# Attention: the causal mask folded into the row-maximum pass, the negated maxima built as diagonals and copied by ScalarE, and a last key block of 16

## The chip, the cores and the metric

The kernel runs on one core of one Trainium2 chip. The metric is the device time of one execution in microseconds (us), the median over the runs. The engines are TensorE (PE; its weight loads are PEld), VectorE (DVE), ScalarE (ACT), GpSimd (POOL) and SyncE (SP), which issues nearly all DMAs from one in-order queue.

## The reference

One layer of a decoder trunk on 1024 tokens plus 16 learned meta tokens (L = 1040, D_MODEL = 1024). An input projection feeds four branches whose gated outputs are summed and projected again. The change lies in the second branch, multi-head latent attention with 8 heads:

```python
k_pos = jnp.arange(lp)
def attend(args):
    qb, i = args
    s = jnp.einsum('bqhd,bkhd->bhqk', qb, k).astype(jnp.float32)
    q_pos = i * Q_BLOCK + jnp.arange(Q_BLOCK)
    s = jnp.where(k_pos[None, :] <= q_pos[:, None], s, -jnp.inf)
    p = jax.nn.softmax(s, axis=-1).astype(v.dtype)
    return jnp.einsum('bhqk,bkhd->bqhd', p, v)
```

Queries and keys have 96 features (64 plus a rotary part of 32), values 64. The softmax is causal; the output leaves out the 16 meta positions.

## The kernel before

The program has three stages. The first, up to about 658 us of the profile, is the input projection (tiles `ps_pa` to `ps_pd`, from split weights `A`, `S` and split inputs `B`, `T`), with the small branches pumped in beside it. The last of these is the norm task of the convolution branch (`lacc`, `cgt`, `bohi`, stores to `bo`). The second, from about 658 to 883 us, is attention together with the output projections of three branches as filler (tiles `ps_y`, operands `bo`, `whl`, `th`, results `m`). The third is the output projection (`ps_u`, `ps_o`).

All float32 matmuls are split into a high and a low part and made of three matmuls. One 512-column matmul moves 128x512.

Attention works on 16 pieces: 8 heads h, each in two halves c of 512 queries. For a piece, `maxima(h, c)` computes each row's maximum first: for four groups of 128 queries the scores of all visible keys in one or two blocks (`ps_s<-kt,qt`, from 144 to 456 columns), the triangular mask `maskS` added on the last 128 columns of the last block, a maximum per block into `mx`, and over the blocks into `mr` (128 queries x 4 groups). `mr` is transposed on PE and spread by a multiplication with `negd` (-1 on a diagonal of 4 groups, 0 elsewhere) into rows 96 to 99 of the query tile `qt`; the key tile `kt` has ones there. So `attend(h, c)` gets scores with the maximum already subtracted. It goes over blocks of 128 keys: three score matmuls (`ps_s<-qt,kt`, keys on the partitions), the mask `maskT` on the diagonal blocks, an exponential on ACT (`p`), a split into high and low (`pt`, ACT and POOL), three matmuls with the values into `ps_o`. The scores of both functions share four PSUM banks (`ps_s`). `ol` is the copy of `ps_o`, `l`, `lc`, `r`, `rb` the row sums' way through DRAM, `lcp` the reciprocals of the last head, which go over PE.

The order on each engine isn't written by hand. The program records its operations, and a list scheduler (`Plan.flush`) walks through them with a cost for each and issues, per engine, the ready operation of the highest priority whose buffers are free. The cost of a PE operation is a rule in `Plan.cost`; these costs set the order only, each engine then runs its own list in that order and waits on semaphores. `plan.ahead` shifts priorities, `plan.behind` holds loads back in the plan. `load_q` and `load_kv` load `qt`, `kt` and `vt`; for heads 0 and 1 the rotary part `kr` is loaded too.

All operations carry line 330 of the profile, where the recorded operations are issued, so the profile is read by tiles.

Of the kernel before, what the change touches and what calls it, by code (L numbers as in the profile page):

```python
# [21 lines left out]
F32 = mybir.dt.float32  # L22
# [171 lines left out]
class Plan:  # L194
# [76 lines left out]
    @staticmethod  # L271
    def cost(eng, op, outs, ins, pow_):
        def size(v):
            return math.prod(v.shape[1:])
        if op == "dma_start":
            v, w = outs[0], ins[0]
            n = math.prod(v.shape) * 4
            run = 4 * min(v.shape[-1], w.shape[-1])
            return {"SP": 450, "ACT": 350, "POOL": 1000}[eng], n * (0.0235 + 35 / run) / 16
        n = max(size(v) for v in outs + [v for v in ins if isinstance(v, View)])  # L280
        if eng == "PE":
            n = size(outs[0])
            return (max(108, n / 2.25 + 3) if op == "transpose" or ins[0].dtype != F32 else max(430, 1.7 * n)), 0
        if eng == "ACT":
            return 200 + 0.83 * n, 0
        if eng == "POOL":
            return (500 + 140 * n if pow_ else 80 + 2.4 * n), 0
        psum = any(isinstance(v, View) and v.buf.psum for v in outs + ins)
        if op == "reciprocal":
            return 150 + 8.5 * n, 0  # L290
        return 142 + (1.2 if op == "scalar_tensor_tensor" and not psum else 1.07) * n, 0
# [144 lines left out]
def trunk_kernel(ctx, tc, a):  # L436
# [816 lines left out]
    for d in range(4):  # L1253
# [2 lines left out]
    boM = [[cp.tile([P, 2, 512], F32R, name=f"boM{i}{c}") for i in range(4)] for c in range(2)]  # L1256
    m_ = [[mpair[c][d // 2][:, d % 2] for d in range(KD)] for c in range(2)]

    maskS = qk.tile([P, P], F32, name="maskS")
    POOL.memset(maskS, 0.0)  # L1260
    POOL.affine_select(out=maskS, in_=maskS, compare_op=ALU.is_ge, fill=NEG,
                       base=0, pattern=[[-1, P]], channel_multiplier=1)
    maskT = qk.tile([P, P], F32, name="maskT")
    POOL.memset(maskT, 0.0)
    POOL.affine_select(out=maskT, in_=maskT, compare_op=ALU.is_ge, fill=NEG,
                       base=0, pattern=[[1, P]], channel_multiplier=-1)

    negd = qk.tile([4, 4, P], F32, name="negd")
    POOL.memset(negd, -1.0)
    POOL.affine_select(out=negd, in_=negd, compare_op=ALU.is_equal, fill=0.0,  # L1270
                       base=0, pattern=[[-1, 4], [0, P]], channel_multiplier=1)
    NA = QK + 4
    qt = {}

# [22 lines left out]
    def maxima(h, c):  # L1297

        q_, k_ = qt[h, c], kt[h % 2]
        mx = at.tile([P, 4, 3], F32, tag="mx", bufs=2, name="mx")
        POOL.memset(mx, NEG)
        for r in range(4):
            nk = NM + P * (4 * c + r + 1)
            nb = -(-nk // 512)
            w_ = -(-nk // nb)
            w_ += w_ % 2
            n0 = 0  # L1310
            for b in range(nb):
                n = min(w_, nk - n0)
                s = bank("s")
                PE.matmul(s[:, :n], q_[:QK, 0, P * r:P * (r + 1)], k_[:QK, 0, n0:n0 + n], start=True, stop=True)
                if b == nb - 1:
                    add(DVE, s[:, n - P:n], s[:, n - P:n], maskS)
                DVE.tensor_reduce(mx[:, r, b:b + 1], s[:, :n], axis=AX.X, op=ALU.max)
                n0 += n
            yield
        mr = at.tile([P, 4], F32, tag="mr", bufs=2, name="mr")  # L1320
        DVE.tensor_reduce(mr, mx, axis=AX.X, op=ALU.max)
        pm = bank("s")
        PE.transpose(pm[:4, :P], mr, ident)
        DVE.tensor_tensor(q_[QK:NA, 0, :].rearrange("p (r n) -> p r n", n=P),
                          pm[:4, :P].unsqueeze(1).to_broadcast([4, 4, P]), negd, op=ALU.mult)
        yield

    ol = {}
# [1 line left out]
    def attend(h, c):  # L1330
# [4 lines left out]
        for j in range(nj):  # L1335
            lo_ = max(512 * c, P * j - NM)
            n = 512 * (c + 1) - lo_
            kn = P if j < 8 else NM
            ks = slice(P * j, P * j + kn)
            qs = slice(512 - n, 512)  # L1340
            s = bank("s")[:kn, :n]
            PE.matmul(s, k_[:NA, 0, ks], q_[:NA, 0, qs], start=True, stop=False)
            PE.matmul(s, k_[:QK, 0, ks], q_[:QK, 1, qs], start=False, stop=False)
            PE.matmul(s, k_[:QK, 1, ks], q_[:QK, 0, qs], start=False, stop=True)
            d0 = P * j - NM
            dl, dh = max(d0, 512 * c, 0), min(d0 + P, 512 * (c + 1))
            if dh > dl:
                sd = s[:, dl - lo_:dh - lo_]
                add(DVE, sd, sd, maskT[:kn, dl - d0:dh - d0])
            p32 = at.tile([P, 512], F32, tag="p32", bufs=3, name="p32")[:kn, :n]  # L1350
            pt_ = at.tile([P, 2, 512], F32R, tag="pt", bufs=4, name="pt")[:kn, :, :n]
            ACT.activation(p32, s, AF.Exp)
            split(pt_[:, 0], pt_[:, 1], p32)
            o = po[:, lo_ - 512 * c:]
            PE.matmul(o, v_[:kn, j, :P], pt_[:, 0], start=(j == 0), stop=False, skip_group_check=True)
            PE.matmul(o, v_[:kn, j, :P], pt_[:, 1], start=False, stop=False, skip_group_check=True)
            PE.matmul(o[:64], v_[:kn, j, P:], pt_[:, 0], start=False, stop=(j == nj - 1), skip_group_check=True)
            yield
# [367 lines left out]
```

## Time and profile before

| what | value |
|---|---|
| runs, us | 1014.47, 1017.25, 1017.0 |
| median, us | 1017.0 |
| span of the profiled execution, us (the page gives no other time for it) | 1016.2 |
| busy share of PE, DVE, ACT, POOL | 98%, 68%, 44%, 67% |
| granted PE clock, mean over the span | 0.994 |
| DMA moved | 203.13 MB, mean 200 GB/s |

In the groups by form a row reads: line, engine, operation, output<-inputs, shapes, count, then busy us and the mean ns of one, then idle time of the engine just before these instructions and what ended it. Matmul durations overlap, so the time that a matmul adds is the distance between two starts. In the timeline a row is start, duration, engine, operation, shapes and count, with idle time before it in brackets.

### The profile page before, as it was taken

The numbers are of one execution on the slowest core, as the hardware profiler recorded it, in microseconds if no ns is written. First come the engines' busy times: TensorE is split into PE (matmuls) and PEld (weight loads), VectorE is DVE, ScalarE is ACT, GpSimd is POOL, SyncE is SP. The second block draws the span as 40 slices with busy tenths as digits, with TensorE's granted clock in tenths as the row PEclk, the third lists the DMA queues.
The fourth block names the chain that finished last, engine by engine and source line by source line (L and its number), as shares of the span: only waits on it lengthen the run. The fifth ranks groups of instructions, "written<-read, shape, count | busy, mean of one in ns | idle before, by whom it ended". The sixth has DMA issues, their size and how long they took to land.

```text
span 1016.2 us, 15260 instructions
## 1 busy us (share of the span) xinstructions
PE 991.6 (98%) x5129; PEld 830.9 (82%) x5129; DVE 689.2 (68%) x1106; ACT 445.3 (44%) x895; POOL 682.1 (67%) x634
## 2 busy tenths in 40 slices
PE   9999999999999999999999999989999999999996
PEld 9999888889888877878778778868887877788885
DVE  6846794897789679645445444166686698699847
ACT  7632233443434545445434344215565546424632
POOL 6768766677566696777668646234589775757946
PEclk9999999999999999999999999999999999999998
DMA  7269756568676866955655633896757671672634
GB/s 246 75 213 298 240 157 193 184 216 293 205 258 207 288 202 199 296 181 160 184 175 187 205 96 114 280 335 203 211 157 250 198 204 58 228 227 84 205 118 165
DMA packets 126302, 203.13 MB, mean 200 GB/s; under 512 B 19650, under 2 KB 79161, under 8 KB 124880
## 3 DMA queue, kind: packets, MB, share of 16 engines
q1 hardware_dynamic: 121600, 185.38, 57.7%
q10 hardware_dynamic: 4336, 15.73, 4.2%
q8 instruction: 40, 0.66, 0.3%
q0 software_dynamic: 288, 1.05, 0.3%
q14 instruction: 38, 0.31, 0.1%
HBM read 128.40 MB, written 73.72 MB: 199 GB/s over the span
## 4 chain that ended last, share of the span: by engine, by line
PE 84%; DMA 5%; DVE 4%; issue 3%; POOL 3%; SPq 0%; ACT 0%; DVEq 0%; POOLq 0%; ACTq 0%
PE ps_pb L330 14%; PE ps_pa L330 14%; PE ps_pc L330 13%; PE ps_o L330 10%; PE ps_s L330 7%; PE ps_u L330 7%; PE ps_pd L330 6%; PE ps_y L330 6%; PE ps_x L330 4%; PE ps_w L330 1%; DMA vt<-v 1%; DMA kt<-kr 1%; DMA th<-th 1%; POOL S L330 1%; DVE ps_w L330 1%
## 5 line engine op out<-in xcount | busy, mean ns | idle before, releaser
L330 PE MATMUL ps_pb<-T,S 128*128 128x512 f32 (+2 forms) x792 | 174.2, 363 | 0.1
L330 PE MATMUL ps_pa<-B,A 128*128 128x512 f32 (+2 forms) x792 | 172.0, 361 | 0.0
L330 POOL TENSOR_TENSOR S<-ss,S 128x512 fp32r<-128x512 f32 x84 | 113.6, 1363 | 72.3 <-ACT S L330 72.2
L330 PEld LDWEIGHTS ps_pa<-B,A 128*128 128x128 f32 x792 | 134.7, 188 | 23.9
L330 PEld LDWEIGHTS ps_pb<-T,S 128*128 128x128 f32 x792 | 133.8, 188 | 24.8 <-issue 1.7
L330 POOL TENSOR_TENSOR A<-raw,A 128x512 fp32r<-128x512 f32 x84 | 114.9, 1377 | 43.7 <-ACT A L330 43.5
L330 POOL TENSOR_TENSOR pt<-p,pt 128x512 fp32r<-128x512 f32 (+4 forms) x112 | 106.2, 972 | 31.4 <-PE ps_s L330 12.7
L330 DVE SCALAR_TENSOR_TENSOR ps_w<-conv,par,ps_w 128x512 f32<-128x512 f32 x116 | 87.3, 752 | 2.6
L330 PE MATMUL ps_pc<-T,S 128*128 128x512 f32 (+2 forms) x396 | 87.8, 363 | 0.5 <-DVE z L330 0.5
L330 PE MATMUL ps_y<-bo,whl 128*128 128x512 f32 x288 | 86.6, 408 | 0.6 <-DVE m L330 0.4
L330 ACT ACTIVATE p<-ps_s 128x512 f32<-128x512 f32 (+4 forms) x112 | 49.8, 445 | 82.9 <-PE ps_s L330 33.0
L330 PE MATMUL ps_pd<-T,A 128*128 128x512 f32 (+2 forms) x396 | 86.0, 362 | 0.0
L330 PE MATMUL ps_pc<-B,S 128*128 128x512 f32 (+2 forms) x396 | 85.8, 362 | 0.0
L330 ACT ACTIVATE S<-ss 128x512 fp32r<-128x512 f32 x84 | 51.0, 628 | 68.7 <-DVE ss L330 38.9
L330 PEld LDWEIGHTS ps_pc<-B,S 128*128 128x128 f32 x396 | 67.3, 188 | 12.3 <-issue 0.5
L330 PEld LDWEIGHTS ps_pd<-T,A 128*128 128x128 f32 x396 | 67.2, 188 | 11.9
L330 PEld LDWEIGHTS ps_pc<-T,S 128*128 128x128 f32 x396 | 66.7, 188 | 12.3 <-DVE z L330 0.7
L330 PE MATMUL ps_s<-qt,kt 100*128 100x512 f32 (+4 forms) x336 | 72.5, 336 | 3.0 <-DVE mx L330 1.5
L330 PE MATMUL ps_o<-pt,vt 128*128 128x512 f32 (+4 forms) x336 | 75.3, 331 | 0.0
L330 PEld LDWEIGHTS ps_s<-qt,kt 100*128 100x128 f32 x336 | 56.9, 186 | 16.0 <-DVE mx L330 3.0
L330 ACT ACTIVATE A<-raw 128x512 fp32r<-128x512 f32 x84 | 52.3, 625 | 34.7 <-PE ps_pd L330 19.3
L330 PEld LDWEIGHTS ps_o<-pt,vt 128*128 128x128 f32 x336 | 52.2, 172 | 12.4 <-POOL pt L330 1.1
(341 smaller groups left out, 1900.4 us busy)
## 6 DMA issues: line engine op xcount, KB each, us to landing
raw<-in_w_in_dram SPq DMA_DIRECT2D x56, 512.0 KB
th<-th SPq DMA_DIRECT2D x32, 512.0 KB
th<-z ACTq DMA_DIRECT2D x30, 512.0 KB
v<-vhl SPq DMA_DIRECT2D x16, 384.0 KB
qt<-q SPq DMA_DIRECT2D x16, 384.0 KB
bo<-bo SPq DMA_DIRECT2D x6, 1024.0 KB
vt<-v SPq DMA_DIRECT2D x8, 768.0 KB
kt<-k SPq DMA_DIRECT2D x8, 520.0 KB
```

The source lines that it names most:

```text
L330: getattr(self.handle[o["eng"]], o["op"])(*map(real, o["args"]), **{k: real(v) for k, v in o["kw"].items()})
```

## The change

It has four parts. The rule that prices PE operations for the scheduler becomes another: a matmul or transpose is priced by the columns of its weights or by the columns that it moves, whichever is more, and a float32 matmul at twice that. In `maxima` the last block's mask addition and maximum become one `tensor_tensor_reduce` over the whole block, for which `maskS` becomes 512 wide (zeros, and the triangle in the last 128 columns). The maxima are multiplied with a small diagonal first (`md`, 128 queries x 4 x 4), each of the four 128x4 pieces is transposed, and ACT copies the 4x512 result into `qt`. In `attend` the last key block of a first half (c = 0) holds the 16 keys that its queries can see rather than 128.

```diff
-            n = size(outs[0])
-            return (max(108, n / 2.25 + 3) if op == "transpose" or ins[0].dtype != F32 else max(430, 1.7 * n)), 0
+            n, m = size(outs[0]), size(ins[0])
+            if op != "transpose" and ins[0].dtype == F32:
+                return 2 * max(6 + 0.82 * m, 0.838 * n), 0
+            return max(6 + 0.82 * m, (0.2 if op == "transpose" else 0.449) * n + 3), 0
...
-    maskS = qk.tile([P, P], F32, name="maskS")
+    maskS = qk.tile([P, 512], F32, name="maskS")
     POOL.memset(maskS, 0.0)
-    POOL.affine_select(out=maskS, in_=maskS, compare_op=ALU.is_ge, fill=NEG,
+    POOL.affine_select(out=maskS[:, 384:], in_=maskS[:, 384:], compare_op=ALU.is_ge, fill=NEG,
                        base=0, pattern=[[-1, P]], channel_multiplier=1)
...
-    negd = qk.tile([4, 4, P], F32, name="negd")
+    negd = qk.tile([P, 4, 4], F32, name="negd")
     POOL.memset(negd, -1.0)
     POOL.affine_select(out=negd, in_=negd, compare_op=ALU.is_equal, fill=0.0,
-                       base=0, pattern=[[-1, 4], [0, P]], channel_multiplier=1)
+                       base=0, pattern=[[1, 4], [-1, 4]], channel_multiplier=0)
...
                 if b == nb - 1:
-                    add(DVE, s[:, n - P:n], s[:, n - P:n], maskS)
-                DVE.tensor_reduce(mx[:, r, b:b + 1], s[:, :n], axis=AX.X, op=ALU.max)
+                    DVE.tensor_tensor_reduce(out=s[:, :n], in0=s[:, :n], in1=maskS[:, 512 - n:], scale=1.0, scalar=NEG,
+                                             op0=ALU.add, op1=ALU.max, accum_out=mx[:, r, b:b + 1])
+                else:
+                    DVE.tensor_reduce(mx[:, r, b:b + 1], s[:, :n], axis=AX.X, op=ALU.max)
...
         DVE.tensor_reduce(mr, mx, axis=AX.X, op=ALU.max)
+        md = at.tile([P, 4, 4], F32, tag="md", bufs=2, name="md")
+        DVE.tensor_tensor(md, mr.unsqueeze(2).to_broadcast([P, 4, 4]), negd, op=ALU.mult)
         pm = bank("s")
-        PE.transpose(pm[:4, :P], mr, ident)
-        DVE.tensor_tensor(q_[QK:NA, 0, :].rearrange("p (r n) -> p r n", n=P),
-                          pm[:4, :P].unsqueeze(1).to_broadcast([4, 4, P]), negd, op=ALU.mult)
+        for r in range(4):
+            PE.transpose(pm[:4, P * r:P * (r + 1)], md[:, r], ident)
+        copy(q_[QK:NA, 0, :], pm[:4])
...
-            kn = P if j < 8 else NM
+            kn = min(P, NM + 512 * (c + 1) - P * j)
```

The new costs move instructions on all engines. Three places show it. The first is DVE behind the tenth piece's last row group: the eleventh piece's first blocks follow. Before, each last block has a mask addition and a reduce:

```order
L330 TENSOR_TENSOR ps_s<-ps_s,maskS 128x128
L330 TENSOR_REDUCE mx<-ps_s 128x1
L330 TENSOR_REDUCE mr<-mx 128x4
L330 TENSOR_TENSOR ps_s<-ps_s,maskS 128x128
L330 TENSOR_REDUCE mx<-ps_s 128x1
L330 TENSOR_TENSOR ps_s<-ps_s,maskS 128x128
L330 TENSOR_REDUCE mx<-ps_s 128x1
L330 TENSOR_TENSOR qt<-ps_s,negd 4x512
```

And after, at the same place (ISA is the fused instruction, and the accumulator read behind it):

```order
L332 ISA ps_s,mx<-ps_s,maskS 128x344
L332 ISA mx 128x1
L332 TENSOR_REDUCE mr<-mx 128x4
L332 TENSOR_TENSOR md<-mr,negd 128x16
L332 ISA ps_s,mx<-ps_s,maskS 128x144
L332 ISA mx 128x1
L332 ISA ps_s,mx<-ps_s,maskS 128x272
L332 ISA mx 128x1
```

Each mask addition is gone, an accumulator read has come, and DVE's pass over `qt` has become a small `md`.

The second place is PE around the same piece's transpose, from its last row group (344 columns) to the next use of `qt`. Before:

```order
L330 MATMUL ps_s<-kt_6740,qt 128x344
L330 MATMUL ps_o<-pt,vt_6749 128x272
L330 MATMUL ps_o<-pt,vt_6749 64x272
L330 MATMUL ps_o<-pt,vt_6749 128x144
L330 MATMUL ps_s<-kt_6860,qt 128x144
L330 MATMUL ps_o<-pt,vt_6749 128x144
L330 MATMUL ps_o<-pt,vt_6749 64x144
L330 MATMUL ps_o<-pt,vt_6749 128x16 x2
L330 MATMUL ps_o<-pt,vt_6749 64x16
L330 MATMUL ps_s<-kt_6860,qt 128x272
L330 MATMUL ps_s<-kt_6860,qt 128x400
L330 MATMUL ps_s<-kt_6860,qt 128x264
```

After the last of these come the transpose `ps_s<-ident,mr`, one block of 264 columns and the first use. In the changed order the last rows ahead of the first use are:

```order
L332 MATMUL ps_s<-kt_6846,qt 128x400
L332 MATMUL ps_y<-bo,whl 128x512 x2
L332 MATMUL ps_s<-kt_6846,qt 128x264
L332 MATMUL ps_y<-bo,whl 128x512
L332 MATMUL ps_o<-pt,vt_6749 128x144
L332 MATMUL ps_o<-pt,vt_6749 64x144
L332 MATMUL ps_o<-pt,vt_6749 128x16 x2
L332 MATMUL ps_o<-pt,vt_6749 64x16
L332 MATMUL ps_s<-ident,md 4x128 x4
L332 MATMUL ps_s<-kt_6846,qt 128x264
L332 MATMUL ps_s<-qt,kt_6740 128x512 x11
```

Three filler matmuls (`ps_y`) have moved in front of the transposes; behind them stands one block of 264 columns, as before.

The third place is the SP queue at the end of the first stage (`raw` are the last weight loads of the input projection, `bo<-bohi` and `bo<-cgt` the norm task's stores). Before:

```order
L330 DMA cgt<-z_cg_2813 128x512
L330 DMA bo_4689<-bohi 128x512
L330 DMA bo_4689<-cgt 128x512
L330 DMA qt<-q_4393 96x1024
L330 DMA kt_6740<-k_2252 64x2080
```

And after:

```order
L332 DMA raw<-in_w_in_dram 128x4x256 x2
L332 DMA bo_4677<-bohi 128x512
L332 DMA bo_4677<-cgt 128x512
L332 DMA raw<-in_w_in_dram 128x4x256 x4
L332 DMA qt<-q_4417 96x1024
L332 DMA kt_6740<-k_2264 64x2080
```

The norm task's stores have moved ahead of the last four weight loads. Further down, seven `th` loads stood ahead of head 1's `kt` before, and six do now.

## The prediction

> **What bounds the kernel now.** I read the page first: shares of the engines, then the chain that ended last.
>
> ```profile
> span 1016.2 us, 15260 instructions
> ...
> PE 991.6 (98%) x5129; PEld 830.9 (82%) x5129; DVE 689.2 (68%) x1106; ACT 445.3 (44%) x895; POOL 682.1 (67%) x634
> ...
> PE 84%; DMA 5%; DVE 4%; issue 3%; POOL 3%; SPq 0%; ACT 0%; DVEq 0%; POOLq 0%; ACTq 0%
> ```
>
> TensorE (PE) is busy for 98% of the span and carries 84% of the chain. So a faster VectorE (DVE) is worth only what PE waits for it, and the change adds nothing large to PE. What can be won is the 1016.2 - 991.6 = 24.6 us in which PE stands, and the time in which its clock is low. The windows view of the attention stage (PE, PEld, DVE, ACT, POOL busy, then the granted clock, DMA share, GB/s) shows where:
>
> ```profile
> 640.00:660.00 20.00, 20.00 (x90) 16.26 (x89) 3.74 (x6) 3.90 (x7) 2.75 (x3) 1.00 0.99 326
> 660.00:680.00 20.00, 18.68 (x81) 14.03 (x80) 13.37 (x32) 2.21 (x5) 5.15 (x13) 1.00 1.04 357
> 680.00:700.00 20.00, 17.36 (x86) 14.07 (x85) 10.58 (x29) 10.50 (x24) 10.32 (x13) 0.91 0.55 155
> ...
> 780.00:800.00 20.00, 18.88 (x93) 14.80 (x91) 12.29 (x33) 10.41 (x23) 15.92 (x20) 0.91 0.74 243
> ...
> sum 260.00, PE 250.40 PEld 203.20 DVE 176.92 ACT 120.66 POOL 159.20; mean PE 19.26 PEld 15.63 DVE 13.61 ACT 9.28 POOL 12.25
> ```
>
> PE stands for 260 - 250.4 = 9.6 us there. In two windows the clock is 0.91, so 0.09 x 20 = 1.8 us of PE's time is lost in each: 3.6 us more. Each dip stands beside a wait, as the view of PE's waits from 640 to 900 us and PE's timeline show (us in total, times, longest; then start, duration, idle before):
>
> ```profile
> PE ps_s L330 <- DVE mx L330: 2.8, 4, 1.5
> PE ps_s L330 <- DMA kt<-kr: 2.6, 1, 2.6
> PE ps_y L330 <- DVE lcp L330: 1.9, 2, 1.2
> PE ps_s L330 <- DVE qt L330: 1.4, 4, 0.4
> ...
> 685.43 0.31 PE L330 MATMUL ps_s<-kt,qt 96*128 96x144 f32 x1 [2.63 <-DMA kt<-kr]
> ...
> 782.74 0.27 PE L330 MATMUL ps_s<-ident,mr 128*4 128x128 f32 x1 [0.39 <-DVE mx L330]
> 783.42 0.39 PE L330 MATMUL ps_s<-kt,qt 96*128 96x264 f32 x1 [0.41 <-DVE mx L330]
> 784.13 3.90 PE L330 MATMUL ps_s<-qt,kt 100*128 100x512 f32 x10 [0.32 <-DVE qt L330]
> ```
>
> The change's own waits are those on mx (row maxima, also what holds the score banks) and qt (negated maxima): 2.8 + 1.4 = 4.2 us, and the dip behind the waits at 782 to 784. The other dip follows the wait for head 1's rotary keys, and that wait comes from the order of the DMA queue, which the change moves too. [...]
>
> **The change part by part.** *Mask and maximum in one.* 64 mask additions (128x128) go; the 64 maxima behind them become a fused instruction and, as the changed order shows, an accumulator read of its own. The groups by form (count | busy, mean ns):
>
> ```profile
> L330 DVE TENSOR_TENSOR ps_s<-ps_s,maskS 128x128 f32<-128x128 f32 x64 | 18.4, 290 | 6.1 <-PE ps_s L330 5.8
> L330 DVE TENSOR_REDUCE mx<-ps_s 128x1 f32<-128x272 f32 x8 | 3.5, 440 | 0.2
> L330 DVE TENSOR_TENSOR z<-ps_pc,u 128x272 f32<-128x272 f32 x10 | 4.4, 440 | 8.4 <-PE ps_pc L330 8.2
> L330 DVE TENSOR_TENSOR m<-m,th 128x512 f32<-128x512 f32 x16 | 16.1, 1008 | 0.4
> L330 DVE TENSOR_REDUCE mr<-mx 128x4 f32<-128x12 f32 x16 | 2.6, 164 | 0.4
> L330 DVE MEMSET ones<- 128x1 f32 x1 | 0.1, 59 | 0.9 <-PEq L1715 0.9
> L330 DVE TENSOR_TENSOR qt<-ps_s,negd 4x512 fp32r<-4x512 f32 x16 | 10.9, 683 | 4.4 <-PE ps_s L330 3.9
> L330 ACT ACTIVATION_READ_ACCUMULATOR junk<-x 128x1 f32 x8 | 1.6, 198 | 0.0
> L330 ACT ACTIVATE ol<-ps_o 128x512 f32<-128x512 f32 x16 | 9.5, 595 | 14.5 <-PE ps_o L330 10.2 <-DVE mr L330 3.0 <-DVE op L330 1.0
> ```
>
> A two-input pass over a score bank costs what a reduce of the same width does (440 ns both at 272), so I price the fused pass as the reduce. No row shows VectorE's accumulator read: between 59 ns (its smallest instruction) and 198 ns (ScalarE's read); I take 164 ns, the tiny reduce, as nearest in kind. Saving: 64 x (290 - 164) = 8.1 us of DVE, with ends 64 x 92 = 5.9 and 64 x 231 = 14.8. If the fused form is slow for a reason no row shows, the worst DVE ratio here is 1008 (m) against 683 (qt) for 512 elements: 48% on a pass of 440 ns is 64 x 0.21 = 13.5 us more, which turns the saving into 5.4 us of loss. [...]
>
> *Negated maxima as diagonals.* 16 DVE passes of 683 ns on 4x512 go; 16 of 128x16 come, priced as 164 ns: 16 x 519 = 8.3 us of DVE. PE gets 48 more transposes, ScalarE 16 copies of 4x512 at 595 ns (the PSUM copy of the same length): 9.5 us on an engine that is busy for 120.66 of the 260 us. Both DVE savings make 16.4 of 176.92 us, 9%.
>
> *Four-column transposes and the key block of 16.* PE's timeline:
>
> ```profile
> 680.12 0.40 PE L330 MATMUL ps_s<-qt,kt 100*128 100x16 f32 x3
> ...
> 742.95 0.23 PE L330 MATMUL ps_s<-qt,kt 100*16 100x16 f32 x3
> ...
> 859.13 0.27 PE L330 MATMUL ps_s<-ident,mr 128*4 128x128 f32 x1
> 859.16 0.72 PE L330 MATMUL ps_y<-bo,whl 128*128 128x512 f32 x2
> ...
> 860.18 1.20 PE L330 MATMUL ps_s<-qt,kt 100*128 100x512 f32 x4 [0.30 <-DVE qt L330]
> ```
>
> The next matmul starts 0.03 us after a transpose with 4 columns: 48 x 0.03 = +1.4 us. Three score matmuls with 128 keys take 0.40, with 16 keys 0.23: in eight first halves 8 x 0.17 = -1.4 us. Sum 0.
>
> *Waits on mx and qt.* Behind the last transpose the first use came 1.05 us later (859.13 to 860.18). The new way is mr, md, transposes, a ScalarE copy instead of mr, transpose, DVE pass: 0.16 more ahead of the transposes, 0.09 less behind, 0.09 of PE; the chain is no shorter, but DVE is less behind and PE's cover is other. At the tenth maxima (the waits at 782 to 784) PE had only score matmuls ahead of the transpose; now three 512-column fillers (0.23 each, 0.7 us) stand there. Counted in the order at the same spacing, PE work from transpose to first use was under 0.5 us at the 1st, 10th, 14th and 16th maxima (0.21, 0.12, 0.12, 0.47); now it is at the 1st and 10th alone (0.21, 0.12). These two cost (1.05 - 0.21) + (1.05 - 0.12) = 1.8, with 0.2 for places near the limit, 2.0 us. So -2.2 us (ends: -4.2 all gone, and 16 x 0.2 = +3 if each copy is late). The dip at 782: the wait there falls from 1.1 to about 0.9 us but from three pieces to one behind one transpose set, so I take it as gone, -1.8 (ends -1.8, 0).
>
> *The order that the new PE costs move.* Ahead of the attention stage SP, an in-order queue, stood at the last store of the norm task, and the loads behind it came late:
>
> ```profile
> 620.43 0.45 SPq L330 DMA_DIRECT2D cgt<-z_cg  x1
> 639.38 0.32 SPq L330 DMA_DIRECT2D bo<-bohi  x1
> 640.76 0.32 SPq L330 DMA_DIRECT2D bo<-cgt  x1
> 641.13 0.42 SPq L330 DMA_DIRECT2D qt<-q  x1
> 641.61 0.51 SPq L330 DMA_DIRECT2D kt<-k  x1
> ...
> 673.81 1.20 SPq L330 DMA_DIRECT2D kt<-kr  x2
> ```
>
> Its DMA rows, for 600 to 640 and for 652 to 677 us (GB/s in 40 slices of each), show idle engines, then full ones:
>
> ```profile
> GB/s 348 194 303 425 389 66 12 0 0 0 0 0 0 0 9 148 355 274 0 287 381 187 302 372 421 139 8 0 0 0 0 16 0 0 0 0 0 0 0 369
> ...
> GB/s 410 433 406 413 403 442 412 408 419 419 354 416 416 406 413 370 429 410 413 403 423 423 419 397 413 416 413 400 400 383 397 397 416 410 367 377 360 347 288 257
> ```
>
> Now the norm task's stores precede the last weight loads, so qt, kt, kr, qt (384 + 520 + 260 + 384 KB, 1.6 MB, 3.8 us at 410 GB/s) can go into the idle stretch. One th (512 KB, 1.25 us) no longer precedes head 1's keys. PE went on 11.6 us after their issue (673.81 to 685.43); 5 us less backlog makes 6.6. Against it PE asks sooner: 54 instead of 63 fillers stand ahead, and from the end of the filler run to the request I count 6.1 us of PE work and, an estimate, 1.5 us of waiting for the first maxima (1.05 behind the transposes, a pass of 0.44 ahead): 7.6. So the 2.6 us wait may vanish; tile releases could keep the loads where they are, so I take -2.0 (ends -2.6, +2), and half of its dip, -0.9. Before 640 us PE's waits are small, this the largest:
>
> ```profile
> PE ps_x L330 <- POOL rs L330: 1.5, 2, 0.8
> ```
>
> The first rs places keep about their cover (18 matmuls become 19, then 21 become 17), the norm ones gain; -0.3 (ends -2, +2). Waits on lcp (1.9) keep their form: 0.
>
> Sum: 0 - 2.2 - 1.8 - 2.0 - 0.9 - 0.3 = -7.2 us. The page gives the profiled execution no time but its span, 1016.2, 0.8 under the median 1017.0 of the runs (1014.47 to 1017.25); I put the difference on the median: 1009.8, say 1010. 0.3% (3 us) is about what these runs can tell from no change.
>
> **The rivals.** *The loads stay.* If qt, kt and vt wait for SBUF that the input stage still holds, the key wait and its dip stay: 1017 - 2.2 - 1.8 - 0.3 = 1012.7. For it: no row shows when that SBUF comes free; against: qt left 0.37 us after the store in front of it (640.76 to 641.13), so it waited for the queue. [...] *Slower by the copy.* ScalarE runs in order; a copy that stands behind two passes of 512 columns (595 ns each, the ol row) is 1.2 us late. Nine of the 16 places have less than 2.25 us between transpose and first use: 9 x 1.2 = 10.8 us against the 7.2 won: 1017 + 3.6 = 1020.6, a new clock dip more 1022. It decides from 6 late copies on. Against it: ScalarE is 46% busy, and it waited 33 us for PE's scores:
>
> ```profile
> ACT p L330 <- PE ps_s L330: 33.0, 8, 4.9
> ```
>
> **How the numbers follow.** Forecast 0.42 (1007 to 1013), loads stay 0.22 (1011 to 1015), no gain 0.21 (1015 to 1019), slower 0.12 (1019 to 1024), better than all ends 0.03. Faster by over 0.3% (under 1014): 0.42 + 0.75 x 0.22 + 0.03 = 0.61 rounded; within: the rest of those and nearly all of no gain, 0.26; slower 0.13. The range leaves out the slower case and the best: 1005.5 to 1018.5.
>
> **What would show it.** Fused rows at about 440 ns for 272 columns and reads under 0.2 us; DVE near 160 us in 640:900; waits on mx and on ScalarE's qt together near 2 us; SP's first qt before 635 and no kr wait; no clock under 1.00 near 782 of the old time. The prediction is wrong if waits on ACT qt pass 4 us, if a key wait over 2 us stands with a dip, or if new waits arise before 640.

## The result, and the profile after

| | median, us | runs | span of the profile, us | mean granted clock |
|---|---|---|---|---|
| before | 1015.84 | 1012.65 to 1018.17 (9) | 1016.2 | 0.994 |
| changed | 1021.59 | 1017.24 to 1023.17 (9) | 1021.5 | 0.991 |

The changed kernel is slower: ratio 1.0055, with a 95% interval of 1.0039 to 1.0070. The prediction said 1010.0 (1005.5 to 1018.5). The profiled execution is the slowest of the nine runs of the changed kernel, and two of the nine lay under 1018 (granted clock 0.993 and 0.995, the other seven 0.989 to 0.992), so what this one trace shows need not be in every run.

The page answers to the rows shown of before:

```profile
span 1021.5 us, 15369 instructions
...
PE 996.7 (98%) x5175; PEld 836.3 (82%) x5175; DVE 667.4 (65%) x1106; ACT 454.6 (44%) x911; POOL 680.6 (67%) x634
```

So does the windows view of the attention stage, the stage as a whole and the stretches with a low clock or a long wait (columns as in the prediction):

```profile
640.00:900.00 260.00, 248.14 (x1267) 201.71 (x1267) 152.75 (x386) 125.21 (x272) 155.66 (x173) 0.97 0.63 194
...
680.00:700.00 20.00, 20.00 (x95) 16.22 (x96) 6.56 (x21) 11.73 (x24) 8.80 (x10) 0.87 0.35 97
...
780.00:800.00 20.00, 19.45 (x107) 16.13 (x106) 11.79 (x34) 13.49 (x28) 18.61 (x18) 1.00 0.81 271
...
820.00:840.00 20.00, 18.69 (x94) 15.11 (x93) 14.25 (x41) 7.81 (x20) 11.30 (x13) 0.91 0.82 225
...
860.00:880.00 20.00, 14.69 (x72) 10.86 (x71) 13.91 (x18) 9.74 (x19) 13.40 (x11) 0.99 0.45 138
880.00:900.00 20.00, 19.04 (x86) 15.32 (x86) 9.83 (x14) 4.46 (x10) 9.61 (x9) 0.92 0.44 155
```

VectorE is busy for 152.75 us instead of 176.92, and yet TensorE stands longer (260 - 248.14 = 11.9 us) and at a lower clock (0.97 instead of 0.99). The dip near 785 is gone; there are dips near 680, 835 and 880 instead. TensorE's waits in the same stretch (total, times, longest):

```profile
PE ps_y L332 <- DVE op L332: 4.9, 1, 4.9
PE ps_s L332 <- DMA kt<-kr: 2.2, 1, 2.2
PE ps_s L332 <- DVE md L332: 1.3, 1, 1.3
PE ps_s L332 <- ACT qt L332: 1.0, 2, 0.6
```

The wait put down to `md` is in part another one. `md` was done at 833.70, but TensorE went on only at 834.30, 0.60 us later; after `op` at the end of the stage it goes on 0.05 us behind the pass it waited for (878.88 + 0.68 = 879.56, then 879.61). The keys of the last head, issued at 823.32, landed at 834.21 by the DMA's semaphore. The dip near 835 follows this wait:

```profile
823.32 0.45 SPq L332 DMA_DIRECT2D kt<-k  x1
...
833.52 0.18 DVE L332 TENSOR_TENSOR md<-mr,negd 128x16 f32<-128x16 f32 x1
...
834.30 0.47 PE L332 MATMUL ps_s<-kt,qt 96*128 96x144 f32 x2 [1.31 <-DVE md L332]
```

The 4.9 us are new. They stand where the attention ends, and the timeline of VectorE, GpSimd and TensorE shows what they come from:

```profile
869.10 2.54 POOL L332 TENSOR_TENSOR op<-op,smg 128x512 f32<-128x512 f32 x2
871.60 2.54 POOL L332 TENSOR_TENSOR boM<-op,boM 128x512 fp32r<-128x512 f32 x2
873.02 5.83 DVE L332 TENSOR_TENSOR m<-m,th 128x512 f32<-128x512 f32 x1
874.11 4.19 POOL L332 TENSOR_TENSOR pt<-p,pt 128x512 fp32r<-128x512 f32 x4
878.88 0.68 DVE L332 TENSOR_TENSOR op<-ol,ps_y 64x512 f32<-64x512 f32 x1
879.61 3.68 PE L332 MATMUL ps_y<-bo,whl 128*128 128x512 f32 x8 [4.91 <-DVE op L332]
```

An addition of 128x512 that otherwise takes 0.69 us takes 5.83: it begins at 873.02 and ends 0.55 us after GpSimd's run of passes (to 874.11 + 4.19 = 878.30). Behind it on VectorE stands `op`, which frees a `ps_y` bank, and TensorE waits for the bank. In before the same additions met GpSimd too, but took at most 1.85 us (1.31 and 1.07 near 870).

The stages part the 5.3 us. The first score matmul of attention and the first matmul behind the stage, in before (L330) and here (L332):

```profile
658.85 0.58 PE L330 MATMUL ps_s<-kt,qt 96*128 96x144 f32 x3
...
883.30 17.03 PE L330 MATMUL ps_u<-boM,whl 128*128 128x512 f32 x72
...
655.10 0.58 PE L332 MATMUL ps_s<-kt,qt 96*128 96x144 f32 x3
...
888.70 3.50 PE L332 MATMUL ps_u<-boM,whl 128*128 128x512 f32 x14
```

The input projection ends 3.75 us sooner; the attention stage, 658.85 to 883.30 before, now takes 233.6 us instead of 224.45, 9.15 more; the output projection is unchanged.

### The profile page after: what moved, and what is told of

Its sections match the earlier page's. It is cut to its first block, busy times and chain, and to the rows that moved or that the text cites. A ratio compares the mean times of both kernels' runs of the same rounds, so it can differ in the third digit from the quotient of the medians.

```text
span 1021.5 us, 15369 instructions
## 1 busy us (share of the span) xinstructions
PE 996.7 (98%) x5175; PEld 836.3 (82%) x5175; DVE 667.4 (65%) x1106; ACT 454.6 (44%) x911; POOL 680.6 (67%) x634
## 4 chain that ended last, share of the span: by engine, by line
PE 94%; DVE 3%; issue 1%; DMA 1%; ACT 1%; SPq 0%; POOL 0%; DVEq 0%; POOLq 0%; ACTq 0%
PE ps_pb L332 16%; PE ps_pa L332 16%; PE ps_pc L332 15%; PE ps_o L332 10%; PE ps_y L332 8%; PE ps_s L332 8%; PE ps_pd L332 8%; PE ps_u L332 7%; PE ps_x L332 4%; PE ps_w L332 1%; DMA kt<-kr 1%; DVE a L332 1%; DVE ps_w L332 0%; DVE c L332 0%; DVE ss L332 0%
## 5 line engine op out<-in xcount | busy, mean ns | idle before, releaser
L332 PE MATMUL ps_pb<-T,S 128*128 128x512 f32 (+2 forms) x792 | 172.8, 362 | 0.8 <-DVE u L332 0.8
L332 PE MATMUL ps_pa<-B,A 128*128 128x512 f32 (+2 forms) x792 | 172.7, 363 | 0.0
L332 POOL TENSOR_TENSOR S<-ss,S 128x512 fp32r<-128x512 f32 x84 | 112.6, 1352 | 82.6 <-ACT S L332 81.2
L332 PEld LDWEIGHTS ps_pa<-B,A 128*128 128x128 f32 x792 | 134.4, 188 | 24.4 <-issue 1.0
L332 PEld LDWEIGHTS ps_pb<-T,S 128*128 128x128 f32 x792 | 133.9, 188 | 24.9 <-DVE u L332 1.2
L332 POOL TENSOR_TENSOR A<-raw,A 128x512 fp32r<-128x512 f32 x84 | 116.2, 1389 | 54.9 <-ACT A L332 47.7
L332 POOL TENSOR_TENSOR pt<-p,pt 128x512 fp32r<-128x512 f32 (+4 forms) x112 | 103.9, 957 | 46.2 <-PE ps_s L332 23.9
L332 PE MATMUL ps_y<-bo,whl 128*128 128x512 f32 x288 | 92.1, 423 | 5.9 <-DVE op L332 4.9
L332 ACT ACTIVATE S<-ss 128x512 fp32r<-128x512 f32 x84 | 50.9, 628 | 105.6 <-DVE ss L332 66.2
L332 DVE SCALAR_TENSOR_TENSOR ps_w<-conv,par,ps_w 128x512 f32<-128x512 f32 x116 | 87.2, 752 | 2.5
L332 PE MATMUL ps_pc<-B,S 128*128 128x512 f32 (+2 forms) x396 | 87.7, 363 | 0.0
L332 PE MATMUL ps_pc<-T,S 128*128 128x512 f32 (+2 forms) x396 | 85.8, 361 | 0.5 <-DVE z L332 0.5
L332 PE MATMUL ps_pd<-T,A 128*128 128x512 f32 (+2 forms) x396 | 85.0, 361 | 0.0
L332 PEld LDWEIGHTS ps_pc<-T,S 128*128 128x128 f32 x396 | 67.1, 188 | 12.5 <-DVE z L332 0.7
L332 PEld LDWEIGHTS ps_pc<-B,S 128*128 128x128 f32 x396 | 66.8, 188 | 12.6 <-issue 1.2
L332 PEld LDWEIGHTS ps_pd<-T,A 128*128 128x128 f32 x396 | 66.8, 188 | 11.8
L332 PE MATMUL ps_o<-pt,vt 128*128 128x512 f32 (+4 forms) x336 | 76.4, 332 | 0.1
L332 PE MATMUL ps_s<-qt,kt 100*128 100x512 f32 (+4 forms) x336 | 69.5, 326 | 1.0 <-ACT qt L332 1.0
L332 ACT ACTIVATE A<-raw 128x512 fp32r<-128x512 f32 x84 | 52.7, 627 | 38.0 <-PE ps_pd L332 23.9
L332 ACT ACTIVATE p<-ps_s 128x512 f32<-128x512 f32 (+4 forms) x112 | 49.7, 443 | 38.6 <-DVE ps_s L332 15.3
L332 PEld LDWEIGHTS ps_s<-qt,kt 100*128 100x128 f32 (+1 forms) x336 | 54.8, 176 | 12.7 <-ACT qt L332 1.1
L332 PEld LDWEIGHTS ps_y<-bo,whl 128*128 128x128 f32 x288 | 53.5, 199 | 14.2 <-DVE op L332 5.3
```

The lines of the kernel that those rows point to most:

```text
L332: getattr(self.handle[o["eng"]], o["op"])(*map(real, o["args"]), **{k: real(v) for k, v in o["kw"].items()})
```

## The experiments

Each kernel was timed beside the kernel before on its own chip, so the ratios are compared, not the medians. "Waits" are TensorE's waits from 640 to 900 us of the profile, "half" the time at half clock up to the last matmul, as the one profiled execution shows them.

| kernel | what it is | median, us | ratio to before (95%) | span | waits | half |
|---|---|---|---|---|---|---|
| before | | | 1 | 1016.2 | 9.3 | 6.8 |
| after | the whole change | 1021.59 | 1.0055 (1.0039 to 1.0070) | 1021.5 | 11.8 | 13.7 |
| c_only | new costs alone | 1010.45 | 0.9960 (0.9947 to 0.9973) | 1007.1 | 7.6 | 3.4 |
| t_only | four transposes and copy alone | 1028.12 | 1.0119 (1.0087 to 1.0152) | 1026.7 | 13.9 | 17.1 |
| all_but_c | change without new costs | 1022.86 | 1.0085 (1.0058 to 1.0111) | 1022.2 | 8.4 | 20.5 |
| all_but_t | change without the transposes | 1015.49 | 1.0008 (0.9993 to 1.0022) | 1011.4 | 8.3 | 3.4 |
| c_3tr | c_only, three idle transposes more | 1016.70 | 1.0027 (1.0010 to 1.0043) | 1015.5 | 7.7 | 6.8 |
| after_split | after, VectorE subtracts in the last piece | 1014.93 | 1.0006 (0.9991 to 1.0021) | 1012.3 | 5.0 | 6.8 |
| cfk_split | the same on all_but_t | 1015.09 | 1.0001 (0.9987 to 1.0015) | 1010.0 | 8.0 | 0 |
| after_psum | after, additions to m from PSUM | 1011.39 | 0.9958 (0.9940 to 0.9976) | 1008.5 | 5.7 | 0 |
| cfk_psum | the same on all_but_t | 1009.93 | 0.9937 (0.9918 to 0.9955) | 1008.4 | 5.3 | 3.4 |
| c_psum | the same on c_only | 1013.59 | 0.9982 (0.9967 to 0.9997) | 1012.0 | 8.2 | 6.8 |
| before_psum | the same on before | 1015.89 | 1.0007 (0.9995 to 1.0020) | 1013.7 | 8.9 | 3.4 |
| ck_pop | ck, products op on GpSimd | 1029.37 | 1.0143 (1.0113 to 1.0173) | 1028.1 | 13.9 | 30.7 |
| cfk_split_pop | cfk_split, products op on GpSimd | 1019.94 | 1.0064 (1.0045 to 1.0083) | 1017.8 | 10.4 | 20.5 |
| cf | new costs, fused maxima | 1013.40 | 0.9998 (0.9987 to 1.0009) | 1012.3 | 7.5 | 13.7 |
| ck | new costs, key block | 1019.26 | 1.0057 (1.0038 to 1.0075) | 1014.2 | 8.9 | 6.8 |
| c_jit | c_only, one cost 2% higher | 1012.06 | 0.9979 (0.9962 to 0.9995) | 1011.1 | 8.4 | 3.4 |
| ck_psum | ck, additions to m from PSUM | 1025.62 | 1.0096 (1.0076 to 1.0116) | 1025.7 | 13.5 | 20.5 |
| cf_psum | cf, additions to m from PSUM | 1016.10 | 1.0009 (0.9995 to 1.0024) | 1013.8 | 9.2 | 10.2 |

### The parts, alone and left out

`c_only` takes the first hunk of the diff and nothing else, `all_but_c` everything but it. `t_only` and `all_but_t` do the same with the hunks of `negd` and `md`:

```diff
+        md = at.tile([P, 4, 4], F32, tag="md", bufs=2, name="md")
+        DVE.tensor_tensor(md, mr.unsqueeze(2).to_broadcast([P, 4, 4]), negd, op=ALU.mult)
         pm = bank("s")
-        PE.transpose(pm[:4, :P], mr, ident)
-        DVE.tensor_tensor(q_[QK:NA, 0, :] ..., pm[:4, :P] ..., negd, op=ALU.mult)
+        for r in range(4):
+            PE.transpose(pm[:4, P * r:P * (r + 1)], md[:, r], ident)
+        copy(q_[QK:NA, 0, :], pm[:4])
```

> The kernel before with nothing but the new rule that prices PE operations. Theory A (TensorE work: four small transposes at 0.109 us instead of one are +5.2 us of TensorE, and the new order by itself is a gain): the input stage ends near 655 us instead of 658.9, the median is 1016 - 3.7 = about 1012, between 1009 and 1014. Theory B (the new order is what costs: the wait of 4.9 us for op near 874 us and two more stretches at half clock come from it): 1020 to 1022, with a wait on op of over 3 us and three or more stretches at half clock.

> The changed kernel with the old rule that prices PE operations, so that the order is near that of before. Theory A: the 5.2 us of transposes stay, the 3.7 us of the input stage (which then ends near 658.9 us) are lost, the shorter waits on the maxima give 2 to 4 back: 1018 to 1022. Theory B: without the new order the loss is gone: 1012 to 1016.5.

> The changed kernel with one transpose per piece and VectorE's pass over qt, as before; fused maxima, key block of 16 and new costs stay. Theory A: 1021.6 - 5.2 = 1016.4, and near 1011 if the wait on op near 874 us goes too; TensorE's attention work 5 us less. Theory B: 1020 to 1022, since the order stays of the new kind and the wait on op and the half-clock stretches with it.

> The kernel before with only the diagonals, the four transposes and ScalarE's copy. Theory A: 64 transposes at 0.109 us instead of 16 are +5.2 us of TensorE, the 8 us that VectorE is relieved of are worth 0 to 2: 1019 to 1022. Theory B: the transposes cost 0.03 us each as the row of before suggests (+1.4) and VectorE's relief gives as much back: 1014 to 1017.5.

Theory A held in all four as to the sign, and B (the new order is what costs) fell: the new costs alone are a gain of 0.4%, and without them the change is no better (1.0085 against 1.0055, the intervals overlap). The first score matmul stands at 654.45 in `c_only` and at 658.87 in `all_but_c`, so the 3.75 us of the input stage belong to the costs. `t_only` missed upwards: 12 us slower by the ratio, where 5.2 were priced. Its profile has the long addition again, with the wait that it brings:

```profile
870.08 6.55 DVE L330 TENSOR_TENSOR m<-m,th 128x512 f32<-128x512 f32 x1
871.38 4.69 POOL L330 TENSOR_TENSOR pt<-p,pt 128x512 fp32r<-128x512 f32 x4
...
877.28 3.78 PE L330 MATMUL ps_y<-bo,whl 128*128 128x512 f32 x8 [5.20 <-DVE th L330]
```

The change's own small pass can be caught in the same way. `md` reads `mr` and `negd`, both in SBUF, while the pass over `qt` that it replaces read one operand from PSUM. It takes 0.18 us, but in `t_only` it stood for 2.55 us during a run of GpSimd's passes, and TensorE waited 1.60 us for the transposes behind it:

```profile
821.11 2.55 DVE L330 TENSOR_TENSOR md<-mr,negd 128x16 f32<-128x16 f32 x1
```

`all_but_c` shows the same collision in another place. Two products `op` stand between a piece's last maximum and its `mr`, TensorE waits for them, and from inside this wait (785.9) on the clock is half for 10.2 us:

```profile
783.80 3.69 DVE L330 TENSOR_TENSOR op<-ol,rb 64x512 f32<-64x512 f32 x2
...
788.11 1.01 PE L330 MATMUL ps_s<-ident,md 128*4 128x128 f32 x4 [3.22 <-DVE mx L330]
```

### What a transpose with four columns costs

In `c_3tr` only transposes are added, into columns that nobody reads:

```diff
-        PE.transpose(pm[:4, :P], mr, ident)
+        for r in range(3, -1, -1):
+            PE.transpose(pm[:4, P * r:P * (r + 1)], mr, ident)
```

> The kernel before with the new costs (c_only), and three more transposes of the row maxima per piece, into columns of the same bank that nobody reads. Nothing changes for VectorE, ScalarE or the data. Theory A (a transpose with 4 columns holds TensorE for 0.109 us, whatever the start of the next matmul says): 48 x 0.109 = +5.2 us against c_only, 1010.5 + 5.2 = 1015.7. Theory of the prediction (0.03 us each): +1.4, 1011.9.

It came out at 1016.7, 0.67 points above `c_only` in the ratio, 6.8 us: the 5.2 us of theory A and not the 1.4 of the prediction. (The profile of `c_3tr` has one stretch at half clock more than that of `c_only`, which is 1.7 us of TensorE's time.) TensorE's timeline (start, duration, count) shows how the one row misled. Before:

```profile
807.07 0.27 PE L330 MATMUL ps_s<-ident,mr 128*4 128x128 f32 x1
807.09 0.95 PE L330 MATMUL ps_y<-bo,whl 128*128 128x512 f32 x3
807.88 0.28 PE L330 MATMUL ps_s<-kt,qt 96*128 96x264 f32 x1
```

And after, at the same piece:

```profile
806.00 0.60 PE L332 MATMUL ps_s<-ident,md 128*4 128x128 f32 x4
806.36 0.71 PE L332 MATMUL ps_y<-bo,whl 128*128 128x512 f32 x2
806.91 0.28 PE L332 MATMUL ps_s<-kt,qt 96*128 96x264 f32 x1
```

In before the filler does start 0.02 us behind the transpose, but the three fillers take 0.79 us where 3 x 0.233 = 0.70 is usual: the other 0.09 of the transpose's 0.11 us is booked to the matmul behind it. Now four in a row show it openly: 0.36 us to the filler, and again 0.08 more in the fillers. A set costs 0.44 instead of 0.11, and 16 x 0.33 = 5.3 us. `c_3tr`'s own rows show the same:

```profile
805.63 0.60 PE L332 MATMUL ps_s<-ident,mr 128*4 128x128 f32 x4
805.98 0.47 PE L332 MATMUL ps_y<-bo,whl 128*128 128x512 f32 x1
```

### The long addition

`after_split` takes GpSimd's passes away from the last piece; `after_psum` leaves GpSimd alone and takes one SBUF operand away from VectorE's 16 additions. `cfk_split`, `cfk_psum`, `c_psum`, `before_psum` are the same edits on the other kernels.

```diff
 after_split
-            split(pt_[:, 0], pt_[:, 1], p32)
+            split(pt_[:, 0], pt_[:, 1], p32, DVE if (h, c) == (H - 1, 1) else None)
 after_psum
-                        DVE.scalar_tensor_tensor(t, t, 1.0, py, op0=ALU.add, op1=ALU.mult)
-                        add(POOL if bi == 1 else DVE, m_[c][d], m_[c][d], t)
+                        o = t if bi == 1 else py
+                        DVE.scalar_tensor_tensor(o, t, 1.0, py, op0=ALU.add, op1=ALU.mult)
+                        add(POOL if bi == 1 else DVE, m_[c][d], m_[c][d], o)
```

> The changed kernel, but in the last piece (head 7, second half) the low part of the exponentials is subtracted on VectorE instead of GpSimd: this takes the row of nine GpSimd passes away behind which VectorE's addition m took 5.83 us, and costs VectorE 9 x 0.69 = 6 us in a stretch in which it is half idle. Theory C (that VectorE pass stands because GpSimd reads SBUF without a gap, and the 4.9 us wait for op and one stretch at half clock follow from it): the pass takes under 2 us, the wait on op is under 1 us, the median 1015 to 1018 with no runs above 1020. Rival D (the tail of the attention is late anyway, the long pass only fills the time): another wait of 3 to 5 us at the same place, 1020 to 1022.

> The changed kernel with VectorE's subtraction in the last piece (after_split, 1014.9) and one transpose per piece as before. Both kernels lack the row of GpSimd passes at the end, so the difference is the price of the transposes with the ScalarE copy alone. Theory A: 5.2 us of TensorE less, 1009.5 to 1010.5. If VectorE's pass over qt (0.68 us, 16 times) brings waits back: 1011 to 1014. If the transposes cost only 0.03 us each: 1013.5 to 1015.

> The changed kernel, but the last 16 gate products th of the filler stay in the PSUM bank, so that VectorE's addition to m has one operand in PSUM instead of two in SBUF. GpSimd's work, its order on the engine and VectorE's number of passes stay. Theory C (only VectorE passes with two SBUF operands stand behind GpSimd): the additions take 0.7 us each, no wait of 4.9 us near 874 us, 1014 to 1017. Rival (any VectorE pass stands while GpSimd runs without a gap, or the pass is long for another reason): one addition of 4 to 6 us stays, 1020 to 1023.

> As after_psum, with one transpose per piece and VectorE's pass over qt as before. The difference to after_psum is what the four transposes with ScalarE's copy cost net, with the long pass out of the way: 5.2 us of TensorE, less what VectorE's relief of 8 us gives back in waits on qt and mx. If nothing is given back: 5 us under after_psum, 1010. If about 3 us are given back, as the waits of cfk_split (8.0 us) and after_split (5.0 us) say: 2 us under it, 1012 to 1014.

> The new costs alone (c_only, 1010.5) with the additions to m from PSUM. The profile of c_only has no pass over 3 us, so little is to be won: 1008.5 to 1011. If the bank that is now held 0.7 us longer makes the filler wait: waits of ps_y on m of 2 us or more, 1011 to 1014.

> The kernel before with the additions to m from PSUM. Its longest addition took 1.85 us, 20 have a median of 0.80, so this saves VectorE about 5 us and TensorE 0 to 2: 1012 to 1014.5. If the longer held bank costs: 1015 to 1017.

Both ways of taking the collision out end the loss: 1.0055 becomes 1.0006 with the passes moved, and 0.9958, a gain of 0.4%, with the operand in PSUM. The one trace showed 6.6 us, the wait and one stretch at half clock. `after_split`, which loads VectorE with about 7 us more, says 5.0 us and `after_psum` 9.9, better than was expected of it (1014 to 1017; it ran in 1011.4). Neither edit leaves the order alone, and the second one's worth elsewhere shows how much that is. It is -7.2 us from `all_but_t` to `cfk_psum` (there an addition of 3.78 us had gone ahead of a wait of 1.5), +2.2 from `c_only`, +0.7 from `before`, +1.1 from `cf` and +3.9 from `ck`. So that the collision is taken out is shown, and that it cost some 5 to 7 us is likely; the 9.9 us are not its price alone. The tile views of `m` (shortest, median, longest pass in ns) are the direct evidence. The changed kernel, with the gate pass that has one operand in PSUM in the first row:

```profile
L332 DVE SCALAR_TENSOR_TENSOR th<-th,ps_y x31: 665/684/690, 736.8 to 885.0; 128x512 f32<-128x512 f32 x31
L332 DVE TENSOR_TENSOR m<-m,th x17: 686/693/5825, 809.4 to 898.1; 128x512 f32<-128x512 f32 x17
```

Before, and then `after_psum`:

```profile
L330 DVE TENSOR_TENSOR m<-m,th x20: 680/744/1850, 820.2 to 898.0; 128x512 f32<-128x512 f32 x20
...
L332 DVE TENSOR_TENSOR m<-m,ps_y x16: 636/686/687, 806.6 to 874.8; 128x512 f32<-128x512 f32 x16
```

In the changed kernel the pass with one operand in PSUM took at most 690 ns and the one with two in SBUF up to 5825; in `after_psum` the same addition with its operand moved to PSUM took at most 687. The addition of 5825 ns stood over five of GpSimd's passes. What decides whether VectorE gets in between two GpSimd passes, as it did in before (additions of 1.31 and 1.07 us, GpSimd's passes then 1.74 us instead of 1.28), is not shown.

`after_psum` against `cfk_psum` gives the net price of the transposes with the collision away: 0.9958 against 0.9937, 2 us of 5.3, as expected with part given back, though the intervals overlap and `cfk_psum` itself came out under its range. `after_split` against `cfk_split` said 0, which the expectation gave as the sign of the small price of 0.03 us. The 5.3 us rest on the starts and on `c_3tr`; that the relief of VectorE pays for 3 to 5 us in both pairs is an inference, for which the waits of 5.0 against 8.0 us in the second pair speak. `c_psum` missed (1013.6; its profile has 8.2 us of waits and 6.8 at half clock where `c_only` has 7.6 and 3.4), and `before_psum` gained nothing (1.0007): where no addition stands long, the edit only moves the order. `cfk_psum` has the lowest ratio found, 0.63% faster than before; its interval overlaps those of `c_only` and `after_psum`.

### Two mends that failed

```diff
-        mul(DVE, op[c][64 * e:64 * (e + 1), :], ol[h][:64, c], rb)
+        mul(POOL if h < H - 1 else DVE, op[c][64 * e:64 * (e + 1), :], ol[h][:64, c], rb)
```

> The kernel with new costs and key block of 16 (ck, 1019.3 against 1013.8 for the kernel before), with the products op of heads 0 to 6 on GpSimd instead of VectorE. In ck two of these passes take 2.3 us on VectorE between the ninth piece's maxima and its qt, TensorE waits 2.8 us for qt near 778 us and then runs 6.8 us at half clock. Theory C (VectorE passes with two operands in SBUF that meet GpSimd's are what the new orders trip over): the wait near 778 is under 0.6 us, no half clock behind it, 1009 to 1013. Rival (the key block itself costs): 1016 to 1020.

> New costs, fused maxima and key block of 16, one transpose per piece, VectorE's subtraction in the last piece and the products op on GpSimd: both places where VectorE met GpSimd are gone. Theory C: no wait over 2 us left but that for head 1's keys, one or two stretches at half clock, 1006 to 1009, better than c_only (1010.5). Rival (GpSimd with 18 us more becomes late with pt): waits of TensorE on POOL pt of over 3 us, 1010 to 1015.

Both came out far above: 1029.4 and 1019.9. Neither the theory's number nor the rivals' mechanism held; the products had left VectorE, but they made GpSimd's runs longer, and an addition stood behind one. The timeline of VectorE, GpSimd and TensorE in `ck_pop`:

```profile
831.34 5.78 DVE L332 TENSOR_TENSOR m<-m,th 128x512 f32<-128x512 f32 x1
832.95 1.25 POOL L332 TENSOR_TENSOR op<-ol,rb 64x512 f32<-64x512 f32 x1
834.88 1.25 POOL L332 TENSOR_TENSOR op<-ol,rb 64x512 f32<-64x512 f32 x1
836.10 0.48 POOL L332 TENSOR_TENSOR pt<-p,pt 128x144 fp32r<-128x144 f32 x1
837.69 0.49 PE L332 MATMUL ps_s<-kt,qt 96*128 96x144 f32 x1 [4.54 <-DVE mx L332]
```

And its windows view right behind, with the clock at 0.75:

```profile
840.00:860.00 20.00, 19.96 (x85) 16.31 (x85) 12.94 (x29) 11.20 (x24) 9.95 (x10) 0.75 0.17 50
```

GpSimd ends at 836.58, the addition at 837.12. The maxima queued behind it keep the score banks, TensorE waits 4.5 us, and 13.7 us at half clock go with it: the mechanism of the changed kernel, brought about in another place by another edit.

### Fused maxima, key block, and the order itself

`cf` and `ck` add one part each to `c_only`; `c_jit` changes 0.449 to 0.46 in its rule; `ck_psum` and `cf_psum` have the additions from PSUM.

> The kernel before with the new costs and the fused maxima only. The runs with and without them so far differ by 5 us (1010.5 with the costs alone, 1015.5 with costs, fused maxima and key block). If the fused pass is what costs: 1014 to 1016, with longer waits of TensorE on mx, qt or the banks. If it is the key block: 1009 to 1011. If neither, but the order that comes out: in between, with waits at other places than the maxima.

> The kernel before with the new costs and the key block of 16 only. By the starts in the traces the score matmuls of a block give back 0.19 us and the value matmuls with 16 keys take about 0.12 us more, in eight first halves: -0.6 us, so 1009 to 1011 if the block itself decides. If the key block is what costs the 5 us: 1014 to 1016.

> The kernel with the new costs alone (c_only, 1010.5), with one number of the rule changed by 2% (0.46 instead of 0.449 ns per column). The operations are the same, only their order moves. If the gain of c_only belongs to the rule (the input stage ends at 655 instead of 659): 1009 to 1012. If half of it is the luck of an order in the attention stage: up to 1015, with the input stage still ending near 655 and the rest in waits and half clock between 760 and 890.

> The kernel with the new costs and the key block of 16 (ck, 1.0057 of the kernel before), with the additions to m from PSUM. If ck is slow through additions that stand behind GpSimd in most of its runs (its profile is of its fastest run and shows none): 1010 to 1014, ratio 0.996 to 1.000. If it is slow through the two products op ahead of qt near 778 us and the half clock behind them, which this leaves as it is: 1016 to 1020.

> cfk_psum (ratio 0.9937) without the key block of 16. By TensorE's starts the block is worth 0.6 us, so if it costs or gives nothing else: 1009 to 1012, ratio 0.993 to 0.997. If the block costs (as ck would have it): under 1008.

The key block, 0.5 us less work for TensorE by the starts (scores -1.5, value matmuls with 16 keys +1.0), moves the ratio by +0.97 points on `c_only` and by -0.72 on `cf_psum`. No price of its own can be read from that. `ck`, `ck_psum` and `cf_psum` came out above all the ranges given for them, so those expectations settle no cause; `cf` came out in between. `ck_psum` tells that the additions are not what makes `ck` slow; left is what its rows show, the two products `op` ahead of `qt`, and in `cf` the same:

```profile
779.26 2.86 DVE L332 TENSOR_TENSOR op<-ol,rb 64x512 f32<-64x512 f32 x2
782.15 0.68 DVE L332 TENSOR_TENSOR qt<-ps_s,negd 4x512 fp32r<-4x512 f32 x1
```

These are the rows of `cf`. TensorE waits 2.8 to 3.0 us there in `cf` and `ck`, and 6.8 us at half clock go with it; in `c_only` the pair stands in the same place, the wait was 1.8 and no dip followed in the profiled run. That the products are the cause of all of `ck`'s loss wasn't shown, since the mend for it made a new collision. `c_jit` kept the early end of the input stage (first score matmul at 655.84) and lies 0.2 points above `c_only`, intervals overlapping: so the gain of the costs held for both numbers tried.

One sum holds over all 20 profiles. Take from each span its waits, half of its time at half clock, and 5.2 us where there are four transposes: what is left lies between 997 and 1003.5 us, where the spans lie between 1007 and 1028. So most of what parts these kernels is waits in the attention stage, the half clock, and the transposes. The end of the input stage, near 659 us under the old costs and at 654.5 to 656.8 under the new, is 2 to 4 us of the rest; what is left beyond that is open.

## Why the prediction was wrong, point by point

In the one profile the terms stand so, half clock counted as half of its time: transposes and key block +4.8, waits on mx and qt -2.8, the dip at 782 -1.7, head 1's keys +1.3, the wait and the dip near 835 +3.0, the collision +6.6, stage one -3.75, other waits -0.5. That is +6.95 where the spans differ by 5.3, so 1.65 us stay unexplained. The forecast was -7.2.

- **The four transposes: the step that failed by size.** "48 x 0.03 = +1.4 us" took the start of the next matmul for the end of the cost; the distance between two starts tells a matmul's price along a run of equal ones, not for one pair. It was 16 x 0.33 = 5.3 us by the starts, and `c_3tr` bears it out (6.8 us by the ratios). The key block's term left out its value matmuls (+1.0). "Sum 0" is +4.8.
- **The cover at the end: the step that was missing.** The prediction counted TensorE's cover between transposes and first use and asked who waits for ScalarE's copy. It did not ask which VectorE passes meet GpSimd, though its own row of `m` (1008 ns for 512 elements against 683) showed that they do; it read it as the price of a slow form. The collision cost some 5 to 7 us, and its place moves with each order.
- **VectorE.** Right: maxima and masks fell from 74.7 us (18.4 + nine rows of 56.3) to 66.2 with the reads, -8.5 where -8.1 was said, and `qt` to `md` from 10.9 to 4.0, -6.9 where -8.3 was said: `md`'s median was 176 ns (164 said), its mean 251, as one of them took 950. Rows of after:

```profile
L332 DVE CUSTOM_DVE_ANT_0 ps_s<-ps_s,maskS 128x272 f32<-128x272 f32 x8 | 3.8, 469 | 0.3 <-PE ps_s L332 0.2
L332 DVE DVE_READ_ACCUMULATOR2_ANT mx<- 128x1 f32 x64 | 9.1, 142 | 0.0
L332 DVE TENSOR_TENSOR md<-mr,negd 128x16 f32<-128x16 f32 x16 | 4.0, 251 | 0.5
L332 ACT ACTIVATE qt<-ps_s 4x512 fp32r<-4x512 f32 x16 | 9.4, 586 | 42.2 <-PE ps_s L332 41.9
```

  The fused pass took 469 ns (440 said), the read 142 (164 said), ScalarE's copy 586 (595 said).
- **Waits on mx and qt.** 4.2 us became 0.4 + 1.0 = 1.4 with ScalarE's `qt`, or 2.7 with the wait near 834 that ended with the keys: -2.8 to -1.5, where -2.2 was said. The dip at 782 went, as said (clock 1.00 from 780 to 800). In before the two dips lasted 3.4 us each and came behind shorter waits: one of 2.6 us, and 1.1 us in three pieces.
- **The rival "slower by the copy"** had the sign right and the mechanism wrong: TensorE waited 1.0 us in all for ScalarE's copy, not 10.8.
- **Head 1's keys: a step that failed too.** The loads did go early, as the order said, but the wait stayed:

```profile
616.10 0.73 SPq L332 DMA_DIRECT2D qt<-q  x1
...
668.21 1.04 SPq L332 DMA_DIRECT2D kt<-kr  x2
...
677.42 0.31 PE L332 MATMUL ps_s<-kt,qt 96*128 96x144 f32 x1 [2.19 <-DMA kt<-kr]
```

  The first `qt` went at 616.1 instead of 641.1, the keys at 668.2 instead of 673.8. TensorE asked 7.6 us sooner (675.2 against 682.8), and the keys landed 9.2 us after their issue, not 6.6: a wait of 2.2 instead of the 0.6 forecast, and 6.8 us at half clock near it, where 3.4 were halved in the forecast. That the last head's keys would be late as well, with a dip of their own near 835, was not in the sum.
- **Stage one.** -0.3 was said, -3.75 came. "The first rs places keep about their cover" was wrong; after has no wait on rs or cqn before 640 us (1.9 + 0.8 before), and `c_only` shows that this is the new costs' doing.

## What to carry to other kernels

Price a short matmul by the distance over which the work behind it returns to its usual pace (0.11 us for a transpose here), not by the start of the next one (0.02 to 0.03). Before moving work between VectorE and GpSimd, list the VectorE passes with two SBUF operands that stand ahead of something the bound engine needs, and give them an operand in PSUM where there is one (here at most 0.69 us instead of up to 5.83); that, with the order that came with it, turned this change from 0.55% slower to 0.4% faster. When a scheduler's costs change the order, time the reordered kernel with each other part taken out in turn, since one part's worth can change its sign with the order (here from +1.0 to -0.7 points).

## What was not expected of the hardware

A single VectorE addition stood for 3.8 to 6.6 us in six kernels (after 5.83, `t_only` 6.55, `ck_pop` 5.78, `cfk_split_pop` 5.62, `cfk_split` and `all_but_t` 3.78), while GpSimd's passes followed each other without a gap (in after from 869.10 to 878.30). In other stretches without a gap the two took turns, as in before near 870 (additions of 1.31 and 1.07 us). The weight load of only four columns was not short either: 4/128 of the 188 ns that a load of 128 columns takes on average (`ps_pa<-B,A`) would be 6 ns, an estimate, but its shortest and median were 81 and 84 ns, and 109 ns lay between two such transposes:

```profile
L332 PEld LDWEIGHTS ps_s<-ident,md x64: 81/84/129, 668.3 to 861.2; 128*4 128x4 f32 x64
```

Whether the load or the pass of 128 columns sets the 109 ns was not tried. A wait went with more lost time than its own length: beside the 4.5 us in `ck_pop` stand 13.7 us at half clock (the mean was 0.91 from 820 to 840 us, 0.75 from 840 to 860), four times the 3.4 us of a dip in before; the first of it began 1.3 us before the wait ended, and it makes some 6 us of TensorE's time.
